# Modulation rows queued behind the feed-forward's weights, and a first stage cut into quarters of the contraction

## Chip, cores and metric

The kernel runs on one core of one Trainium2 chip, in one launch. The metric is device time in microseconds. Times inside the profile are counted from the start of the span of one profiled execution.

## What is computed

Two transformer blocks over 256 tokens of width 1024, in fp32 accuracy. The first block has two layers; in each, a modulation (adaLN) vector made from a condition `c` scales and shifts the normed input:

```python
def adaln(cond, w_mod, b_mod):
    m = jnp.dot(jax.nn.silu(cond), w_mod) + b_mod
    return jnp.split(m[..., None, :], 6, axis=-1)
...
for l in range(DEPTH):                        # DEPTH = 2
    sh1, sc1, g1, sh2, sc2, g2 = adaln(c, w_mod[l], b_mod[l])
    csh1, csc1, cg1, csh2, csc2, cg2 = adaln(c_ctx, w_mod[l], b_mod[l])
    h = modulate(rms_norm(x, norm1_g[l]), sh1, sc1)
    hc = modulate(rms_norm(xc, norm1_g[l]), csh1, csc1)
    q, k, v, up, ca, cb = project_inputs(h, w_in[l], q_norm_g[l], k_norm_g[l])
...
    mix = jnp.concatenate([attn, pool_o, conv_o], axis=-1)
    x = x + g1 * jnp.einsum('blm,md->bld', mix, w_out[l])
    x = x + g2 * swiglu(modulate(rms_norm(x, norm2_g[l]), sh2, sc2), w_ffn_in[l], w_ffn_out[l])
```

Here `modulate(h, shift, scale)` is `h * (1 + scale) + shift`, and `w_mod[l]` is 1024 by 6144. Layer 0 does the same for the context `xc`. The second block (four gated branches) is the same in both kernels.

## The kernel before

**Layout.** Activations lie feature-major: 8 tiles of 128 features, with 512 columns (256 context tokens, 256 tokens). Every product is made of three fp32r matmuls (`mm3`, L353 to L355): high times high, high times low, low times high. `weights` loads a chunk of 512 KB into one of 4 `wraw` buffers (an issue on SP), rounds it on ScalarE (`whi`, L343) and takes the rest on VectorE (`wlo`, L344); `whi` and `wlo` have 3 buffers each.

**Order.** The program is traced in order, and a scheduler then orders each engine's instructions by the readiness that it works out at build time and by priority (earlier in the trace is higher). Work that waits for nothing can so be moved far ahead of its place. `tc.issue_after(i)` holds every instruction traced in its block on i's engine, and only there, behind i in that engine's queue.

**First stage of layer 0.** `modulation` makes a group of 1024 modulation columns: 8 chunks of `w_mod` (128 rows by 1024 columns, 512 KB), four matmuls of 256 columns for each (L507), then a copy, two transposes (L514) and additions of the bias. Groups 0 and 1 hold shift and scale of features 0 to 511 and 512 to 1023. `first_norm(0)` makes group 0 and norms features 0 to 511 (`norm`, L489 to L492). Then `feats` runs the first three of the four products of the convolution's input (`ab`, each 128 columns by the whole contraction) over the first half of the contraction, with the steps of `first_norm(1)` in between, and over the second half after it. The fourth product follows alone. The row of reciprocal norms that `norm` needs comes from L431 to L474.

**Rest of the modulation.** Layer 0's other three PE groups lie in `queue`; `fill` steps them from `each`, twice for each of the first 12 of 16 attention units, with the lower priority `LATE`. Layer 0's last part and all six of layer 1 come from `modulation_by_rows` on VectorE: a transposed chunk of `w_mod` (512 KB, in one of 2 `wmod` buffers) is multiplied with the row of silu(c) and summed (L567), for each of up to two conditions, after the condition's rows have been loaded and put through Silu (L559). It is a generator that is stepped three times for each feed-forward unit of layer 0; one step is one chunk with all its conditions, 56 steps in all.

**After attention** come the merge (`project_rows`, L867 and L881, with L835 as the residual), the second norm (L442, L446, L489 to L492), and the feed-forward in thirds of 8, 7 and 7 units.

Of the kernel before, what the change touches and what calls it, by code (L numbers as in the profile page):

```python
# [39 lines left out]

MOD_GROUPS = {0: ((4, 5, 0, 1), (6, 7, 2, 3)) + tuple(tuple(range(4 * i, 4 * i + 4)) for i in (2, 4, 3))}
# [12 lines left out]
def _weight_plan():  # L54
# [7 lines left out]
    for l in range(DEPTH):  # L62
        for g, parts in enumerate(MOD_GROUPS.get(l, ())):
            cols = np.concatenate([np.arange(c * 256, c * 256 + 256) for c in parts])
            for k in range(8):
                rows(("mod", l, g, k), "w_mod", (l,), cols, k * 128, 1)
        for which in range(6):
# [17 lines left out]
        for j in range(4):  # L85
# [190 lines left out]
def tile_two_blocks(ctx: ExitStack, tc: tile.TileContext, w: bass.AP, blk: bass.AP, cols: bass.AP,  # L276
# [61 lines left out]
    def weights(key):  # L338
# [4 lines left out]
        act.copy(out=hi[:, :m], in_=t[:, :m])  # L343
        dve.tensor_tensor(lo[:, :m], t[:, :m], hi[:, :m].bitcast(F32), op=ALU.subtract)  # L344
# [24 lines left out]
    def feats(items, h, spans, between=None, p="mm"):  # L369

# [4 lines left out]
        turns = [range(KD)] if between is None else [range(KD // 2), range(KD // 2, KD)]  # L375
        behind = None
        n = 0
        for a, b in spans:
            for ks in turns:
                if ks[0]:  # L380
                    behind = None
                for (wH, wL), t in zip(ws, ps):
                    for k in ks:
                        with tc.issue_after(behind.ins) if behind else nullcontext():
                            mm3(t[:, a - lo:b - lo], (wH[:, k], wL[:, k]), (h[0][:, k, a:b], h[1][:, k, a:b]),
                                k == 0, k == KD - 1)
                        n += 1
                        if between and n in STEPS:
                            for _ in range(STEPS[n]):
                                behind = next(between, behind)  # L390
# [86 lines left out]
    def norm(h, lo, hi, parts, ks=range(KD), row=None, wide=False):  # L477

        ps, bc = row or rows_of_rstd(lo, hi)
        for k in ks:  # L480
            for a, b, sc, sh in parts:
# [9 lines left out]
                act.activation(hi_, t, AF.Identity, bias=sh[:, k:k + 1])  # L491
                dve.scalar_tensor_tensor(lo_, t, sh[:, k:k + 1], hi_.bitcast(F32), op0=ALU.add,  # L492
# [6 lines left out]
    modv = {l: const.tile([128, 6, KD, 2], F32, name=f"modv{l}") for l in range(DEPTH)}  # L499

# [43 lines left out]
    def fill(n):  # L544
# [3 lines left out]
        for _ in range(n):  # L548
            while queue and next(queue[0], None) is None:
# [1092 lines left out]
```

## Time and profile before

| what | us |
|---|---|
| three runs | 1454.83, 1464.14, 1463.14; median 1463.14 |
| profiled execution, device time | 1457.94 |
| its span, first to last instruction | 1455.8 |
| PE busy in the span | 1367.4 (94%) |
| VectorE, ScalarE, GpSimd busy | 959.2, 623.2, 233.3 |

PE is TensorE's matmul queue. Busy time of PE is modelled from starts; what counts is where PE stands idle and at which granted clock it runs (PEclk 1.00 is 2.4 GHz, 0.50 would be 1.2 GHz throughout; its mean over the span is 0.957). 2.1 us of the device time lie outside the span.

### The profile page before, as it was taken

The numbers are of one execution on the slowest core, as the hardware profiler recorded it, in microseconds if no ns is written. First come the engines' busy times: TensorE is split into PE (matmuls) and PEld (weight loads), VectorE is DVE, ScalarE is ACT, GpSimd is POOL, SyncE is SP. The second block draws the span as 40 slices with busy tenths as digits, with TensorE's granted clock in tenths as the row PEclk, the third lists the DMA queues.
The fourth block names the chain that finished last, engine by engine and source line by source line (L and its number), as shares of the span: only waits on it lengthen the run. The fifth ranks groups of instructions, "written<-read, shape, count | busy, mean of one in ns | idle before, by whom it ended". The sixth has DMA issues, their size and how long they took to land. (4 is left out here: it accounts for less than half of the span.)

```text
span 1455.8 us, 22714 instructions
## 1 busy us (share of the span) xinstructions
PE 1367.4 (94%) x8750; PEld 1195.1 (82%) x8750; DVE 959.2 (66%) x1924; ACT 623.2 (43%) x1100; POOL 233.3 (16%) x274
## 2 busy tenths in 40 slices
PE   5999989879999999998988989999989998999999
PEld 2699656778878888888967889999967887988999
DVE  4598659998784333335986755555695676657565
ACT  3333464242212222324444544434654559446443
POOL 0055530230000000003416210000362002000000
PEclk9999977989999999999978999999998999999999
DMA  9632533437773223222321335555642423434553
GB/s 341 227 127 92 191 137 107 159 118 259 261 251 124 95 95 102 96 92 74 124 80 44 103 130 189 177 186 178 235 150 94 153 84 109 133 109 150 184 181 129
DMA packets 61308, 213.51 MB, mean 147 GB/s; under 512 B 6928, under 2 KB 8080, under 8 KB 60944
## 3 DMA queue, kind: packets, MB, share of 16 engines
q1 hardware_dynamic: 60768, 209.90, 42.6%
q10 hardware_dynamic: 432, 2.16, 0.4%
q8 instruction: 69, 1.13, 0.3%
q14 instruction: 39, 0.32, 0.1%
HBM read 210.98 MB, written 1.05 MB: 146 GB/s over the span
## 5 line engine op out<-in xcount | busy, mean ns | idle before, releaser
L343 ACT CAST whi<-wraw 128x1024 fp32r<-128x1024 f32 (+2 forms) x296 | 304.7, 1033 | 515.5 <-PE ps_mm L354 256.6
L344 DVE TENSOR_TENSOR wlo<-wraw,whi 128x1024 fp32r<-128x1024 f32 (+2 forms) x296 | 360.6, 1220 | 181.9 <-ACT whi L343 179.2
L353 PE MATMUL ps_mm<-hH,whi 128*128 128x256 f32 (+1 forms) x1056 | 345.0, 330 | 10.4 <-ACT hH L491 7.3
L354 PE MATMUL ps_mm<-hL,whi 128*128 128x256 f32 (+1 forms) x1056 | 343.1, 326 | 1.9 <-DVE hL L492 1.9
L355 PE MATMUL ps_mm<-hH,wlo 128*128 128x256 f32 (+1 forms) x1056 | 342.2, 325 | 1.3 <-DVE wlo L344 1.3
L353 PEld LDWEIGHTS ps_mm<-hH,whi 128*128 128x128 f32 x1056 | 204.6, 195 | 32.3 <-ACT hH L491 9.1
L353 PE MATMUL ps_mm<-hidH,whi 128*128 128x256 f32 (+1 forms) x683 | 216.9, 320 | 7.7 <-ACT hidH L349 4.8
L354 PEld LDWEIGHTS ps_mm<-hL,whi 128*128 128x128 f32 x1056 | 205.1, 194 | 19.6 <-DVE hL L492 3.4
L355 PEld LDWEIGHTS ps_mm<-hH,wlo 128*128 128x128 f32 x1056 | 204.9, 194 | 17.1 <-DVE wlo L344 1.9
L354 PE MATMUL ps_mm<-hidL,whi 128*128 128x256 f32 (+1 forms) x683 | 216.2, 317 | 2.4 <-DVE hidL L350 2.3
L355 PE MATMUL ps_mm<-hidH,wlo 128*128 128x256 f32 (+1 forms) x683 | 215.3, 317 | 0.1
L354 PE MATMUL ps_mm<-wlo,hH 128*128 128x256 f32 (+2 forms) x464 | 145.8, 316 | 4.9 <-DVE wlo L344 4.9
L353 PEld LDWEIGHTS ps_mm<-hidH,whi 128*128 128x128 f32 x683 | 130.3, 192 | 17.8 <-ACT hidH L349 5.7
L353 PE MATMUL ps_mm<-whi,hH 128*128 128x256 f32 (+2 forms) x464 | 141.2, 313 | 2.0 <-ACT tm L634 1.5
L355 PE MATMUL ps_mm<-whi,hL 128*128 128x256 f32 (+2 forms) x464 | 142.9, 310 | 0.0
L354 PEld LDWEIGHTS ps_mm<-hidL,whi 128*128 128x128 f32 x683 | 130.9, 192 | 12.2 <-DVE hidL L350 3.5
L355 PEld LDWEIGHTS ps_mm<-hidH,wlo 128*128 128x128 f32 x683 | 130.5, 192 | 8.7 <-DVE wlo L344 0.5
L567 DVE CUSTOM_DVE_ANT_0 ps_md<-wmod,tm 128x512 f32<-128x512 f32 x160 | 114.7, 717 | 21.8 <-DMA wmod<-in_w_dram 19.9
L464 POOL TENSOR_TENSOR squares<-squares,scr 128x256 f32<-128x256 f32 (+1 forms) x28 | 31.6, 1129 | 567.3 <-ACT scr L463 566.9
L358 POOL TENSOR_TENSOR st<-st,mhalf 128x4 f32<-128x4 f32 (+3 forms) x54 | 69.3, 1289 | 224.0 <-DVE st L619 95.8
L354 PEld LDWEIGHTS ps_mm<-wlo,hH 128*128 128x128 f32 x464 | 89.6, 193 | 13.4 <-DVE wlo L344 7.6
L353 PEld LDWEIGHTS ps_mm<-whi,hH 128*128 128x128 f32 x464 | 88.7, 193 | 7.4 <-ACT tm L634 1.6
(346 smaller groups left out, 1996.4 us busy)
## 6 DMA issues: line engine op xcount, KB each, us to landing
wraw<-in_w_dram SPq DMA_DIRECT2D x271, 512.0 KB, 3.4
wmod<-in_w_dram SPq DMA_DIRECT2D x85, 512.0 KB, 4.0
wraw<-in_w_dram SPq DMA_DIRECT2D x32, 448.0 KB, 3.2
xT<-in_x_dram ACTq DMA_DIRECT2D x2, 1024.0 KB, 6.8
single<-in_w_dram SPq DMA_DIRECT2D x8, 256.0 KB, 7.6
wraw<-in_w_dram SPq DMA_DIRECT2D x4, 288.0 KB, 3.2
tm<-in_rows_dram SPq DMA_DIRECT2D x4, 256.0 KB, 6.0
out_dram<-scr SPq DMA_DIRECT2D x8, 128.0 KB, 1.7
```

Of the source, the lines that this page charges most:

```text
L343: act.copy(out=hi[:, :m], in_=t[:, :m])
L344: dve.tensor_tensor(lo[:, :m], t[:, :m], hi[:, :m].bitcast(F32), op=ALU.subtract)
L353: pe.matmul(ps, a[0], b[0], start=start, stop=False)
L354: pe.matmul(ps, a[0], b[1], start=False, stop=False)
L355: P["product"] = pe.matmul(ps, a[1], b[0], start=False, stop=stop)
L358: pool.tensor_tensor(t, t, mhalf[:, :n], op=ALU.pow)
L464: eng.tensor_tensor(squares[:, lo:hi], squares[:, lo:hi], q, op=ALU.add)
L567: dve.tensor_tensor_reduce(bank("md"), t[:, i * 512:i * 512 + 512], crow[2 * j + i], 1.0, 0.0, ALU.mult, ALU.add, sums[j][:, i * KD + d:i ...
```

## The change

- The first stage goes by quarters of the contraction. The first two modulation groups are replaced by four parts (`first_modulation`), each with shift and scale of 256 features: 4 chunks of two row blocks by 512 columns (512 KB), eight matmuls of 128 columns for each chunk, one copy, one transpose. The four `ab` products take their weights as four chunks of 256 rows by 512 columns (`abq`) and accumulate in four banks side by side. After the products of each of a quarter's two feature tiles, two chunks of the next part are stepped, behind the last product on PE (`P["product"]`).
- The first weights after that stage are rounded and split behind the last norm of it (`P["behind"]`), and `layer_scalars` is held behind the same norm and the last product.
- `fill` is held behind the last product traced before it.
- The rows on VectorE: one step is one chunk with one condition (80 steps). They are stepped three times for each feed-forward unit and once for each output tile of the feed-forward's projection, VectorE's part behind the last weights' split (`P["split"]`), the loads behind the last load (`P["load"]`).

```diff
-ROWS_PER_STEP = 3
+ROWS_PER_STEP = (3, 1)
-STEPS = {1: 1, 2: 1, 3: 1, 4: 1, 5: 1, 6: 1, 7: 1, 8: 1, 11: 9}
-MOD_GROUPS = {0: ((4, 5, 0, 1), (6, 7, 2, 3)) + tuple(tuple(range(4 * i, 4 * i + 4)) for i in (2, 4, 3))}
+MOD_GROUPS = {0: tuple(tuple(range(4 * i, 4 * i + 4)) for i in (2, 4, 3))}
...
+        if l == 0:
+            for q in range(4):
+                cols = np.arange(q * 256, q * 256 + 256)
+                for k in range(0, 8, 2):
+                    rows(("first", q, k), "w_mod", (l,), np.concatenate([D + cols, cols]), k * 128, 2)
+                rows(("abq", q), "w_in", (l,), np.arange(1792, 2304), q * 256, 2)
...
-        act.copy(out=hi[:, :m], in_=t[:, :m])
-        dve.tensor_tensor(lo[:, :m], t[:, :m], hi[:, :m].bitcast(F32), op=ALU.subtract)
+        with ExitStack() as order:
+            for i in P.pop("behind", ()):
+                order.enter_context(tc.issue_after(i.ins))
+            act.copy(out=hi[:, :m], in_=t[:, :m])
+            P["split"] = dve.tensor_tensor(lo[:, :m], t[:, :m], hi[:, :m].bitcast(F32), op=ALU.subtract)
...
+    def first_modulation(q, pools, p):
+        ps = bank(p)
+        for k in range(0, KD, 2):
+            t = raw_chunk(("first", q, k), next(pools))[0]
+            for i in range(2):
+                for g in range(4):
+                    o = i * 512 + g * 128
+                    pe.matmul(ps[g * 32:g * 32 + 32, :128], csil[:, k + i, :], t[:, o:o + 128],
+                              start=(k + i == 0), stop=(k + i == KD - 1), tile_position=(0, g * 32))
+            yield
+        cp = P["wk"].tile([128, 256], F32, name="cp")[:, :128]
+        act.copy(out=cp, in_=ps[:, :128])
+        pe.transpose(ps[:, 256:384], cp, ident)
...
-        for _ in range(n):
-            while queue and next(queue[0], None) is None:
-                queue.pop(0)
+        with tc.issue_after(P["product"].ins):
+            for _ in range(n):
+                while queue and next(queue[0], None) is None:
+                    queue.pop(0)
...
+    def rows_step(i):
+        with tc.issue_after(P["split"].ins), tc.issue_after(P["load"].ins):
+            for _ in range(ROWS_PER_STEP[i]):
+                next(rows, None)
...
-                if d < KD - 1:
-                    yield
+                    if d < KD - 1 or j < js[-1]:
+                        yield
...
+    def first_products(items):
+        pools = cycle(("wraw", "wraw", "wmod"))
+        ps = [bank("mm" if i < 3 else "sc") for i in range(4)]
+        mods = [first_modulation(q, pools, ("md", "sc")[q % 2]) for q in range(4)]
+        for q in range(4):
+            wH, wL = weights(("abq", q))
+            for _ in mods[q]:
+                pass
+            norm(h, 0, 512, parts(0, 0, scale1, (0, 1)), range(2 * q, 2 * q + 2), row, True)
+            for k in range(2):
+                for (key, _), t in zip(items, ps):
+                    c = slice(key[2] * 128, key[2] * 128 + 128)
+                    mm3(t, (wH[:, k, c], wL[:, k, c]), tuple(x[:, 2 * q + k] for x in h), q + k == 0, q + k == 4)
+                if q < 3:
+                    with tc.issue_after(P["product"].ins):
+                        next(mods[q + 1])
+                        next(mods[q + 1])
+        P["behind"] = P["normed"], P["rest"]
+        for (_, evac), t in zip(items, ps):
+            evac(t)
...
-        layer_scalars(l)
+        with tc.issue_after(P["normed"].ins), tc.issue_after(P["rest"].ins), tc.issue_after(P["product"].ins):
+            layer_scalars(l)
...
-                if not last:
-                    for _ in range(ROWS_PER_STEP):
-                        next(rows, None)
+                rows_step(0)
...
             project_rows(l, range(KD), lambda d: (weights(("fo", l, t, d)), hs), range(f1 - f0), 5, final, 1, lo,
-                         after2 if final else None)
+                         after2 if final else None, lambda: rows_step(1))
```

## Rows read from the trace of the kernel before

**Rows 1.** Windows: us; PE, PEld, DVE, ACT, POOL busy (count); PEclk; DMA share; GB/s.

```profile
190.00:200.00 10.00, 7.21 (x42) 5.19 (x34) 2.08 (x6) 9.87 (x20) 6.91 (x10) 0.67 0.50 181
200.00:210.00 10.00, 10.00 (x30) 5.52 (x28) 6.80 (x20) 3.82 (x11) 0.00 (x0) 0.68 0.01 2
...
280.00:300.00 20.00, 13.66 (x95) 12.13 (x93) 19.94 (x48) 6.95 (x13) 7.04 (x8) 0.96 0.49 166
300.00:320.00 20.00, 18.37 (x121) 18.12 (x122) 20.00 (x52) 7.09 (x16) 10.48 (x10) 0.78 0.29 99
...
340.00:360.00 20.00, 20.00 (x90) 16.57 (x89) 16.88 (x42) 6.18 (x8) 0.00 (x0) 1.00 0.77 259
...
660.00:680.00 20.00, 16.73 (x130) 16.33 (x129) 10.78 (x21) 7.72 (x15) 6.76 (x8) 0.94 0.33 107
680.00:700.00 20.00, 19.44 (x143) 18.89 (x142) 16.93 (x32) 12.66 (x22) 9.56 (x8) 0.89 0.26 83
```

**Rows 2.** Instructions of L567 over the whole span; duration ns, first and last start.

```profile
L567 DVE CUSTOM_DVE_ANT_0 ps_md<-wmod,tm x160: 683/699/1730, 202.7 to 440.0; 128x512 f32<-128x512 f32 x160
L567 DVE DVE_READ_ACCUMULATOR2_ANT st<- x160: 133/140/146, 203.3 to 440.6; 128x1 f32 x160
...
  DMA wmod<-in_w_dram: 19.9, 20
```

**Rows 3.** Instructions of L559 over the whole span.

```profile
L559 ACT ACTIVATE tm<-tm x4: 629/630/637, 187.1 to 195.9; 128x512 f32<-128x512 f32 x4
L559 ACT ACT_TABLE_LOAD  x3: 1283/1283/1283, 185.8 to 194.6; - x3
```

**Rows 4.** Timeline of PE, 150 to 240: start, us, line, operation, count, idle before.

```profile
157.54 0.38 PE L353 MATMUL ps_sc<-hidH 64*128 64x256 f32 x1
...
170.23 0.39 PE L355 MATMUL ps_sc<-hidH,hidL 64*128 64x512 f32 x1
...
189.74 1.08 PE L507 MATMUL ps_md<-wmod,csil 128*32 128x256 f32 x8 [3.44 <-DMA wmod<-in_w_dram]
...
200.22 0.79 PE L353 MATMUL ps_sc<-hidH 64*128 64x512 f32 x1
...
232.28 0.62 PE L355 MATMUL ps_sc<-hidH,hidL 64*128 64x512 f32 x1
```

**Rows 5.** Timeline of PE, 262 to 310.

```profile
290.35 0.39 PE L353 MATMUL ps_mm<-hidH,whi 128*128 128x256 f32 x1 [1.48 <-DVE xT L835]
...
298.10 0.77 PE L446 MATMUL ps_aux<-scr,ones 128*128 128x256 f32 x2 [3.72 <-DVE scr L442]
...
301.22 0.80 PE L353 MATMUL ps_mm<-hH,whi 128*128 128x256 f32 x2 [2.36 <-ACT hH L491]
```

**Rows 6.** Groups of VectorE by line, 280 to 325: busy us, mean ns, idle before.

```profile
L567 DVE CUSTOM_DVE_ANT_0 ps_md<-wmod,tm 128x512 f32<-128x512 f32 x30 | 24.1, 805 | 0.1
```

**Rows 7.** Timeline of PE and ACT, 19 to 66.

```profile
19.75 2.08 PE L446 MATMUL ps_aux<-scr,ones 128*128 128x512 f32 x2
...
23.06 0.37 ACT L512 COPY cp<-ps_sc 128x256 f32<-128x256 f32 x1 [0.60 <-PE ps_sc L507]
...
27.26 0.50 PE L353 MATMUL ps_mm<-hH,whi 128*128 128x512 f32 x1 [3.34 <-ACT hH L491]
...
46.47 0.64 PE L507 MATMUL ps_md<-wmod,csil 128*32 128x256 f32 x8
...
64.23 0.39 PE L354 MATMUL ps_mm<-hL,whi 128*128 128x512 f32 x1
64.46 0.39 PE L355 MATMUL ps_mm<-hH,wlo 128*128 128x512 f32 x1
```

**Rows 8.** Window 20 to 40; columns as in Rows 1.

```profile
20.00:40.00 20.00, 14.42 (x87) 6.37 (x88) 10.64 (x25) 7.41 (x13) 0.35 (x1) 0.83 0.94 323
```

**Rows 9.** Groups of PE by line and shape, 0 to 64.

```profile
L507 PE MATMUL ps_md<-wmod,csil 128*32 128x256 f32 x32 | 3.0, 389 | 0.0
```

**Rows 10.** The page's costliest groups.

```profile
L344 DVE TENSOR_TENSOR wlo<-wraw,whi 128x1024 fp32r<-128x1024 f32 (+2 forms) x296 | 360.6, 1220 | 181.9 <-ACT whi L343 179.2
```

More of the change, by code (lines that the diff above doesn't have):

```diff
@@ L84, in _weight_plan @@
             rows(("up", l, j), "w_in", (l,), np.arange(1536 + j * 128, 1664 + j * 128), 0, 8)
-        for j in range(4):
+        for j in range(4 if l else 0):
             rows(("ab", l, j), "w_in", (l,), np.arange(1792 + j * 128, 1920 + j * 128), 0, 8)
@@ L367, in st, with feats @@
         return P["wk"].tile([128, n], F32, name=f"st{n}", bufs=8 if n < 64 else 3)
-    def feats(items, h, spans, between=None, p="mm"):
+    def feats(items, h, spans, p="mm"):
         ws = [weights(key) for key, _ in items]
@@ L374, in feats @@
         lo, hi = min(a for a, b in spans), max(b for a, b in spans)
-        turns = [range(KD)] if between is None else [range(KD // 2), range(KD // 2, KD)]
-        behind = None
-        n = 0
         for a, b in spans:
[L379 to L390, printed above, removed]
+            for (wH, wL), t in zip(ws, ps):
+                for k in range(KD):
+                    mm3(t[:, a - lo:b - lo], (wH[:, k], wL[:, k]), (h[0][:, k, a:b], h[1][:, k, a:b]),
+                        k == 0, k == KD - 1)
         for (key, evac), t in zip(items, ps):
@@ L490, in norm @@
                 hi_, lo_ = h[0][:, k, a:b], h[1][:, k, a:b]
[L491 to L492 removed]
+                P["normed"] = act.activation(hi_, t, AF.Identity, bias=sh[:, k:k + 1])
+                P["rest"] = dve.scalar_tensor_tensor(lo_, t, sh[:, k:k + 1], hi_.bitcast(F32), op0=ALU.add,
                                          op1=ALU.subtract)
@@ L845, in tile_two_blocks, with project_rows @@
     h = new_h()
-    pools = cycle(("wraw", "wraw", "wmod"))
-    def first_norm(half):
-        yield from modulation(0, half, pools, "sc")
-        norm(h, 0, 512, parts(0, 0, scale1, (0, 1)), range(half * 4, half * 4 + 4), row, True)
-    for _ in first_norm(0):
-        pass
-    def project_rows(l, d_list, make, ks, which, final, first_half, lo, after):
+    def first_products(items):
[18 more added lines that the diff above has]
+            evac(t)
+    def project_rows(l, d_list, make, ks, which, final, first_half, lo, after, each=None):
         late = d_list[-3:] if lo == 0 and final else ()
@@ L870, in project_rows @@
                 after(d, lo, 512)
+            if each:
+                each()
         if not late:
@@ L883, in project_rows @@
                 after(d, s * 256, s * 256 + 256)
+    rows = modulation_by_rows()
     for l in range(DEPTH):
@@ L891, in tile_two_blocks @@
         if not last:
-            queue.extend(modulation(0, g) for g in range(2, 5))
+            queue.extend(modulation(0, g) for g in range(3))
         mix = {}
@@ L975, in tile_two_blocks @@
         project_rows(l, range(KD), lambda d: merge(1, d), range(4), 2, True, 0, lo, after)
-        rows = modulation_by_rows() if not last else None
         for t, (f0, f1) in enumerate(THIRDS):
```

14 lines of the change are left out of this document (12 added, 2 removed).

## Prediction

> **What bounds the kernel now.** I read the page's busy times first, then windows of 20 us over the span, then the waits and the timeline wherever PE was not full. PE is busy 94% of the span, so time is won only where PE idles or runs at the low clock. The steady feed-forward is not such a place: from 340 to 360 PE shows 20.00 of 20 at clock 1.00, although VectorE is at 16.88 and carries modulation rows [rows 1]. The rows are L567: 160 instructions of 0.70 us with 160 reads of 0.14 us, 134 us of VectorE in all, started from 202.7 to 440.0 [rows 2]. Their place in the trace is the feed-forward, yet they begin in the middle of attention: the scheduler used them as filler. Silu of the condition went along: four Silu and three table loads between 185.8 and 196.5, among the exponentials [rows 3]; each return to Exp is another load.
>
> Four places lose PE time. (a) From 190 to 200 PE is busy 7.21 of 10 at clock 0.67 while ScalarE is at 9.87; just before, PE stands 3.44 us at a queued modulation matmul whose chunk has not landed [rows 1, 4]. (b) From 200 to 233 attention runs with rows between its VectorE steps, at clock 0.68 [rows 1, 4]. (c) From 280 to 320 VectorE is 99.7% busy and PE loses 8.0 us (6.34 and 1.63); the chain of the second norm waits 1.48, 3.72 and 2.36 us [rows 1, 5], and 24.1 us of VectorE there are rows [rows 6]. (d) The first stage, which ends at 64.9 [rows 7].
>
> **(a) Silu and the fills.** Silu moves into the feed-forward, whose gate uses the same function. The three loads of 1.283 us, as many back to Exp, and 4 times 0.63 us leave ScalarE's queue, 10.2 us in all [rows 3]. PE can get back at most its idle 2.8 us, the wait of 3.44 us, and half of the low-clock time: clock 0.67 means that 66% of 10 us ran at 1.2 GHz, so 3.3 us. Sum 9.5; the floor is 0, if attention's chain fills the gap. I take 4, since the DMA wait may only move: the fills stay two for each unit, but now behind the unit's product instead of wherever the scheduler put them. Behind a waiting fill the unit's own matmuls still stand. Their loads are issued ahead on SP, one unit before, so I expect less waiting, not more.
>
> The Trainium skill (ScalarE: Activation LUTs, section "What ACT_TABLE_LOAD costs") adds a drain of about 1.38 us to each load, 2.66 us for a switch. Between the starts of the first and the third Silu load lie four switches (two to Silu, two back), 10.6 us by that figure, more than the 8.8 us that the rows leave; the rows speak for 1.28.
>
> **(b) Rows out of attention.** From 157.54 to 170.62 eight score products, four units, take 13.1 us: 3.3 us for a unit, without rows. From 200.22 to 232.90 twelve, six units, take 32.7 us, 5.4 for a unit [rows 4]. The excess of 2.1 us times six is 12.6 us, and the rows do not part its causes: matmuls of pooling and of the convolution's norm that stand in the second stretch, PE at 1.2 GHz, and attention's steps standing behind rows of 0.84 us. If it is only the first two, the gain is 0. I take a third, 4.
>
> **(c) Rows out of the norm.** After the change a row's VectorE part stands behind the split of the last weights traced, and the fourth weights of the feed-forward need one of three `whi` buffers, so no row can come before the first products. What remains is like the boundary from layer 0 to layer 1, which has no rows: 660 to 700 loses 3.27 and 0.56 us [rows 1]. Against 8.0 that gives 4.1 us. Low clock: 8% and 44% of 20 us before (10.4 us), 12% and 22% there (6.8 us); half the difference is 1.8 us. Sum 5.9. GpSimd's additions of squares then show up, as they do there, so I take 5; bounds 3 and 8.
>
> **(d) First stage by quarters.** Bytes and products stay: 16 chunks of 512 KB, 96 products. Products start 0.23 us apart [rows 7], so a quarter's 24 cost 5.5 us. A chunk was eight matmuls of 256 columns, 0.64 us [rows 7]; now it is sixteen of 128 columns. It costs between the same (columns decide) and twice that, 1.28 (instructions decide); I take 0.9, nearer to the row, so 3.6 us for a part. At each seam PE has nothing else: the part's last chunk is queued behind the quarter's last product, and copy, transpose, bias, scale and norm must follow. Before, copy to first product took 4.2 us (23.06 to 27.26), with a weight split of 1.2 us on VectorE in the way [rows 7, 10]; now that split lies under the products. I take 3.0. A quarter is 5.5 + 3.6 + 3.0 = 12.1; three and a last 5.5 make 41.8.
>
> The start: only a quarter's modulation (2 MB instead of 4) stands ahead, so the row of norms decides. Its broadcast L446 ended at 21.8 [rows 7]; the norm's two passes and the rounding, an estimated 0.9 us, put the first product at 22.7, against 27.26. End: 64.5 against 64.9. Before, the stage also did four fill steps (32 matmuls, 3.0 us) [rows 9], which now go into attention, where PE has idle time. Against this stands the clock: before, after an idle of 3.34 us, 20 to 40 ran at 0.83 [rows 7, 8], 34% of 20 us low, 3.4 us lost. Three seams of 3 us may each cost half of that or all. I set 3 us won against 3 us lost: 0, bounds 6 us won and 17 lost (below). The evacuations now come together at the end; the first finishes its Sigmoid under the other three products, so a bank is free in time. `layer_scalars` and the first split behind the last norm delay nothing that PE wants at once.
>
> **(e) Where the rows go.** 80 steps: three for each of 7, 7 and 7 units, and one for each projection tile: 29 by the end of the first third, 58 by the end of the second, 80 early in the last projection. The gate needed first (16 steps) is ready before the first projection. One unit gets 3 times 1.68 = 5.0 us of VectorE where before it got up to 10. Loads per unit on SP are 1.5 to 3 as before, with the same two buffers, and the four small loads of the condition's rows go along; a row waiting for its load now holds up the next weight split. Before, VectorE stood so 20 times, 19.9 us in all [rows 2], and PE stayed full [rows 1]. Cost 0; if that cover went, up to 3.
>
> **Sum.** 4 + 4 + 5 + 0 - 0 = 13 us. From the profiled execution's 1457.9 this gives 1445. That execution lies 5.2 us under the median of the three runs; the four executions average 1460.0, and from this I predict 1447. They spread over 0.64%, so 1% is about what can be told from no change.
>
> **Rivals.** *Attention is set by PE at 1.2 GHz.* Then (b) gives nothing and (a) only about 2: 7 us, 1453. For it: PE shows 10.00 of 10 from 200 to 210 at 0.68. Against it: from 190 to 200 the clock is as low with PE idle for 28% of the time, so there it follows the waiting and not the reverse [rows 1].
>
> *The seams keep the clock low (slower).* If PE runs from the second quarter on at 1.2 GHz, 72 products cost 0.23 us more each (16.6), and the eight chunks between them 0.9 more each (7.2): 23.8 us, less the 6 that an early start and the moved fills can win, so 17 net (rounded down). Against 13 won elsewhere that is 4 slower: 1464. It decides once the extra passes 19 us, four fifths of that. For it: 3.72 us of idle at 298 is followed by 0.78 in the next window [rows 1, 5]. Against it: each quarter holds 9 us of unbroken products. The Trainium skill (TensorE: Matmul & The Clock Gate, section "Why this matters for your kernels") warns against idle gaps between bursts of matmuls because they return the engine to its low clock; it speaks against this change at three seams, and no row here shows gaps repeated like this.
>
> *Attention returns to 2.4 GHz.* With Silu and rows gone, units take near 3.3 us again from 185 on: (a) and (b) give some 16 of their 22 us, (c) its 5, and the time is 1439. For it: four units ran so until 170 [rows 4]. Against it: the second stretch also holds other matmuls that stay.
>
> *The hold does nothing*, because the scheduler still finds room for rows early: then at most (a)'s fills count, 4 us, 1456. The fourth weights' wait for a buffer speaks against it.
>
> **Chances.** Forecast 0.50 (1440 to 1453), attention set by the clock 0.20, seams 0.12, attention at full clock 0.13, hold without effect 0.05. The range runs from 1434 (full clock and a good first stage) to 1463. More than 1% faster is below 1448.5 against the median and below 1445.4 against the mean of the four; between these, the forecast's range lies below in about half of its cases (0.27), and the full-clock case adds 0.13: 0.40. Slower by over 1% needs the seams at their worst and little won elsewhere: 0.06. Within 1%: 0.54.
>
> **What would show it.** Right: L567 starts after the first feed-forward product and runs to the end of layer 0; no table load for Silu among the exponentials; PE idle from 280 to 320 halved; first product before 24; three gaps of about 3 us in the first stage. Wrong: the stage ending later than 68 or its windows under clock 0.9; PE waiting on `wlo` in the feed-forward; attention as long as before with VectorE free.

## The result, and the profile after

The changed kernel takes 1442.24 us (median of 1445.26, 1442.25, 1442.22 and 1440.2), against 1459.12 of the kernel before beside it on the chip: ratio 0.9885, 95% interval 0.984 to 0.993. Its profiled execution has a span of 1443.5 us, 12.3 less than before's 1455.8.

Where they went is read from five starts on PE's timeline that both kernels have. Of the kernel before, first qk product, first merge product, and the first sum of squares of layer 1 (the first product at 27.26 and the first feed-forward product at 301.22 stand in [rows 7, 5]):

```profile
64.69 0.40 PE L353 MATMUL ps_mm<-whi,hH 128*128 128x256 f32 x2
...
236.93 1.42 PE L353 MATMUL ps_mm<-hidH,whi 128*128 128x512 f32 x1
...
666.68 0.28 PE L431 MATMUL ps_aux<-ones,squares 128*128 128x1 f32 x2
```

Of the changed kernel, the same view, with the transposes (L510) and first products (L361) of the first stage's quarters. A seam is PE's wait between a quarter's transpose and its first product, here 3.58, 5.61 and 1.91 us:

```profile
24.52 0.50 PE L361 MATMUL ps_mm<-hH,whi 128*128 128x512 f32 x1 [1.99 <-ACT hH L487]
...
28.82 0.95 PE L505 MATMUL ps_sc<-wraw,csil 128*32 128x128 f32 x16
29.59 0.61 PE L505 MATMUL ps_sc<-wmod,csil 128*32 128x128 f32 x16
30.13 0.50 PE L361 MATMUL ps_mm<-hH,whi 128*128 128x512 f32 x1
...
34.60 0.33 PE L510 MATMUL ps_sc<-first,cp 128*128 128x128 f32 x1 [0.44 <-ACT cp L509]
38.50 1.65 PE L361 MATMUL ps_mm<-hH,whi 128*128 128x512 f32 x3 [3.58 <-ACT hH L487]
...
49.06 0.33 PE L510 MATMUL ps_md<-first,cp 128*128 128x128 f32 x1 [0.44 <-ACT cp L509]
55.00 1.65 PE L361 MATMUL ps_mm<-hH,whi 128*128 128x512 f32 x3 [5.61 <-ACT hH L487]
...
65.84 0.33 PE L510 MATMUL ps_sc<-first,cp 128*128 128x128 f32 x1 [0.44 <-ACT cp L509]
68.08 0.97 PE L361 MATMUL ps_mm<-hH,whi 128*128 128x512 f32 x3 [1.91 <-ACT hH L487]
...
74.19 0.39 PE L361 MATMUL ps_mm<-whi,hH 128*128 128x256 f32 x1
...
162.74 0.45 PE L731 MATMUL ps_aux<-first,e 128*128 128x128 f32 x1 [2.10 <-DVE hidL L358]
...
239.15 0.79 PE L361 MATMUL ps_mm<-hidH,whi 128*128 128x512 f32 x1
291.56 0.38 PE L361 MATMUL ps_mm<-hH,whi 128*128 128x256 f32 x1 [2.19 <-ACT hH L487]
```

Layer 1 begins at 651.39. From start to start:

| stretch, us | before | after | difference |
|---|---|---|---|
| to the first product | 27.26 | 24.52 | -2.7 |
| first stage, to the first qk product | 37.43 | 49.67 | +12.2 |
| attention, to the first merge product | 172.24 | 164.96 | -7.3 |
| merges and second norm, to the first feed-forward product | 64.29 | 52.41 | -11.9 |
| feed-forward of layer 0 | 365.46 | 359.83 | -5.6 |
| the rest of the span | 789.1 | 792.1 | +3.0 |

The change is two changes with opposite signs. With the rows away from attention and the norm, three stretches win 24.8 us; the first stage by quarters ends 9.5 us later than before. The last row holds none of the moved work (of the edits only the hold on layer 1's `layer_scalars` reaches it): over all the profiled executions below that part takes 788 to 797 us, with and without that hold.

Windows of the changed kernel, columns as in [rows 1]:

```profile
20.00:40.00 20.00, 13.99 (x104) 8.96 (x97) 9.19 (x23) 6.64 (x13) 0.00 (x0) 0.82 0.59 207
40.00:60.00 20.00, 13.95 (x99) 10.34 (x97) 5.60 (x14) 3.03 (x6) 1.52 (x3) 0.76 0.66 214
...
160.00:180.00 20.00, 17.71 (x100) 11.76 (x92) 12.92 (x31) 9.11 (x30) 10.97 (x22) 0.66 0.49 164
180.00:200.00 20.00, 19.27 (x122) 11.65 (x120) 11.58 (x23) 8.62 (x25) 9.22 (x16) 1.00 0.50 177
200.00:220.00 20.00, 18.50 (x123) 11.32 (x122) 13.07 (x35) 9.88 (x30) 6.05 (x9) 1.00 0.41 136
...
280.00:300.00 20.00, 17.48 (x116) 16.78 (x115) 12.87 (x26) 10.19 (x21) 11.17 (x12) 0.83 0.36 135
300.00:320.00 20.00, 20.00 (x142) 18.75 (x141) 13.72 (x27) 9.62 (x17) 4.29 (x4) 1.00 0.21 67
```

From 180 to 220 the clock is 1.00, where before had 0.67 and 0.68 from 190 to 210 [rows 1]; from 280 to 320 PE loses 2.52 us instead of 8.0 and VectorE has room. Against that, 20 to 60 stands at 0.82 and 0.76, and attention has a fall of its own: 0.66 from 160 to 180, behind the wait of 2.10 us at 162.74.

The rows, L595, over the span, and the Silu of the condition, L587:

```profile
L595 DVE CUSTOM_DVE_ANT_0 ps_md<-wmod,tm x160: 689/699/702, 313.7 to 612.7; 128x512 f32<-128x512 f32 x160
...
  DMA wmod<-in_w_dram: 9.9, 13
```
```profile
L587 ACT ACTIVATE tm<-tm x4: 631/632/633, 278.0 to 281.3; 128x512 f32<-128x512 f32 x4
```

The hold works: no row before 313.7, and none in the last 38 us of layer 0. The Silus run in the second norm, with no table load of their own.

### The profile page after: what moved, and what is told of

Its sections match the earlier page's. It is cut to its first block, busy times and chain, and to the rows that moved or that the text cites. A ratio compares the mean times of both kernels' runs of the same rounds, so it can differ in the third digit from the quotient of the medians.

```text
span 1443.5 us, 22992 instructions
## 1 busy us (share of the span) xinstructions
PE 1360.8 (94%) x8878; PEld 1197.9 (83%) x8878; DVE 965.6 (67%) x1928; ACT 614.5 (43%) x1094; POOL 237.8 (16%) x274
## 5 line engine op out<-in xcount | busy, mean ns | idle before, releaser
L361 PE MATMUL ps_mm<-hH,whi 128*128 128x256 f32 (+1 forms) x1056 | 344.3, 330 | 18.9 <-ACT hH L487 16.9
L361 PEld LDWEIGHTS ps_mm<-hH,whi 128*128 128x128 f32 x1056 | 204.3, 195 | 39.5 <-ACT hH L487 19.6
L361 PE MATMUL ps_mm<-hidH,whi 128*128 128x256 f32 (+1 forms) x683 | 214.8, 317 | 3.0 <-ACT hidH L357 1.7
L361 PE MATMUL ps_mm<-whi,hH 128*128 128x256 f32 (+2 forms) x464 | 141.1, 313 | 2.0 <-ACT tm L662 1.5
L361 PEld LDWEIGHTS ps_mm<-hidH,whi 128*128 128x128 f32 x683 | 129.2, 190 | 12.0 <-ACT hidH L357 1.9
L595 DVE CUSTOM_DVE_ANT_0 ps_md<-wmod,tm 128x512 f32<-128x512 f32 x160 | 111.5, 697 | 12.7 <-DMA wmod<-in_w_dram 9.9
L863 DVE SCALAR_TENSOR_TENSOR xT<-ps_mm,modv,xT 128x256 f32<-128x256 f32 x116 | 52.6, 480 | 72.5 <-PE ps_mm L363 72.4
```

Source lines behind the costliest of these rows:

```text
L361: pe.matmul(ps, a[0], b[0], start=start, stop=False)
L595: dve.tensor_tensor_reduce(bank("md"), t[:, i * 512:i * 512 + 512], crow[2 * j + i], 1.0, 0.0, ALU.mult, ALU.add, sums[j][:, i * KD + d:i ...
L863: dve.scalar_tensor_tensor(xT[:, d, r], ps[:, s * 256 - lo:s * 256 - lo + 256], M(l, which, 1 - s)[:, d:d + 1], xT[:, d, r], op0=ALU.mult, ...
```

## Experiments

Each kernel is timed beside the kernel before; "stage", "attention", "norm" and "FFN" are the stretches of the table above in its one profiled execution, "wait" is the longest idle of PE within attention that the timeline shows, and "at 0.50" is how much of attention ran at that granted clock, in us, from windows cut where the clock changes.

| kernel | median us | ratio (95%) | stage ends | attention | wait | at 0.50 | norm | FFN | span |
|---|---|---|---|---|---|---|---|---|---|
| before | 1459.12 | 1 | 64.69 | 172.24 | 3.44 | 33.9 | 64.29 | 365.46 | 1455.8 |
| after | 1442.24 | 0.9885 (0.984 to 0.993) | 74.19 | 164.96 | 2.10 | 20.5 | 52.41 | 359.83 | 1443.5 |
| rows_only | 1428.25 | 0.9803 (0.9781 to 0.9824) | 64.15 | 155.53 | 1.42 | 4.2 | 52.82 | 360.09 | 1424.9 |
| quarters_only | 1476.87 | 1.0148 (1.0108 to 1.0188) | 80.65 | 177.98 | 2.68 | 43.0 | 65.30 | 368.54 | 1485.5 |
| rows_fill | 1431.23 | 0.9818 (0.979 to 0.9846) | 62.73 | 160.84 | 1.32 | 19.6 | 55.99 | 360.22 | 1429.9 |
| abq_early | 1443.72 | 0.9907 (0.9876 to 0.9938) | 73.22 | 162.62 | 2.18 | 21.9 | 56.39 | 360.51 | 1443.9 |
| silu_back | 1440.98 | 0.9884 (0.9827 to 0.9941) | 64.08 | 167.70 | 2.06 | 27.3 | 53.99 | 359.77 | 1441.4 |
| rows_norm | 1447.35 | 0.9928 (0.9898 to 0.9958) | 64.28 | 157.49 | 1.83 | 13.7 | 65.21 | 366.14 | 1441.2 |
| hidden | 1434.12 | 0.9837 (0.9782 to 0.9892) | 60.46 | 162.20 | 2.18 | 25.3 | 53.40 | 359.63 | 1430.5 |
| after_unheld | 1445.07 | 0.9917 (0.9888 to 0.9947) | 79.47 | 163.53 | 1.98 | 18.9 | 52.22 | 359.80 | 1443.5 |
| hidden_free | 1431.57 | 0.9832 (0.9792 to 0.9872) | 61.75 | 158.10 | 1.32 | 12.7 | 54.41 | 358.73 | 1422.8 |
| hidden_unheld | 1433.75 | 0.9834 (0.9788 to 0.9881) | 64.96 | 167.29 | 1.83 | 28.1 | 52.67 | 358.29 | 1440.3 |
| silu_once | 1437.58 | 0.9863 (0.982 to 0.9905) | 64.42 | 166.93 | 2.07 | 27.3 | 53.97 | 359.76 | 1434.4 |
| rows_only_again | 1434.03 | 0.9826 (0.9793 to 0.9859) | 64.26 | 154.47 | 1.39 | 0.4 | 55.68 | 359.35 | 1430.1 |

### The two halves of the change

**rows_only**: the kernel before with the rows' part of the diff.

```diff
-ROWS_PER_STEP = 3
+ROWS_PER_STEP = (3, 1)
...
-                if not last:
-                    for _ in range(ROWS_PER_STEP):
-                        next(rows, None)
+                rows_step(0)
...
+            if each:
+                each()
```

`rows_step(0)` is three steps, `each` in `project_rows` is `rows_step(1)`, one step; both stand behind the last split and load.

> The kernel before with the rows alone changed: begun behind the feed-forward's weights, three steps a pair and one an output tile; its first stage and its unheld fill steps stay. If the parts add up (theory: the rows won about 25 us and the first stage by quarters gave back about 9.5 of it), the first qk product stays at 64.7 us, the first feed-forward product comes 15 to 25 us earlier than before's 301.2, and the whole takes 1434 to 1444 us, faster than the changed kernel or level with it. If the prediction's sum was right piece by piece (rows and Silus 13, first stage 0), it takes about 1446 us. If the hold on the fill steps was the larger part of the gain in attention, attention stays as long as before (172 us from first qk product to first merge product) and only the 8 to 12 us of the second norm are won: about 1449.

Measured 1428.25 us, faster than the changed kernel, and more than the 25 us of the first theory. Its windows:

```profile
160.00:180.00 20.00, 18.58 (x134) 11.86 (x131) 12.89 (x31) 7.56 (x25) 11.50 (x28) 1.00 0.50 165
180.00:200.00 20.00, 18.90 (x125) 12.87 (x122) 16.00 (x35) 12.44 (x38) 12.11 (x15) 1.00 0.32 101
200.00:220.00 20.00, 16.01 (x83) 11.47 (x81) 15.46 (x41) 13.22 (x41) 2.02 (x2) 0.89 0.00 1
```

Attention stays at 1.00 nearly to its end and takes 155.53 us, 16.7 less than before; the norm wins 11.5 and the feed-forward 5.4.

**quarters_only**: the changed kernel with the rows and the fill steps as before.

```diff
-        with tc.issue_after(P["product"].ins):
-            for _ in range(n):
+        for _ in range(n):
...
-                rows_step(0)
+                if not last:
+                    for _ in range(ROWS_PER_STEP):
+                        next(rows, None)
```

> The changed kernel with before's rows (three steps a pair, free to run ahead into attention) and its fill steps unheld: what is left of the change is the first stage by quarters. If the seams are a loss that nothing returns, the first qk product comes 6 to 10 us later than before's 64.7 and the whole is slower by that: 1465 to 1469 us. If the prediction's term was right (0, within 6 won and 17 lost, the seams paid by the earlier first product), 1459. If the later end of the first stage is given back in attention because the rows and the fill steps that ran inside the first stage before now find time there, between the two, and attention is shorter by what the stage is longer.

Measured 1476.87, slower by 1.5%: the first stage by quarters alone is a loss, and nothing returns it. That is more than the 1465 to 1469 expected. The stage ends 16.0 us later than before's, not 6 to 10, with seams of 5.51 and 6.24 us and a fill step in front of the last quarter that stands 3.28 us for its chunk. (The profiled execution, 1487.30, is the slowest of the four.) The product of the two halves' ratios, 0.9948, is above the whole change's 0.9885; neither half has the hold on the fill steps, which the next two runs look at.

**rows_fill**: rows_only with the hold on the fill steps.

```diff
-        for _ in range(n):
-            while queue and next(queue[0], None) is None:
+        with tc.issue_after(P["product"].ins):
+            for _ in range(n):
+                while queue and next(queue[0], None) is None:
```

> The kernel before with the rows changed and the fill steps of the modulation held behind the products, its first stage as before. If the parts add up: first qk product near 65 us, first feed-forward product near 282 (before's 301.2 less about 7 in attention and 12 in the norm), and the whole 1430 to 1436 us, about 9 us faster than the changed kernel. If the first stage by quarters costs nothing, or frees attention of fill steps that are back here, it is level with the changed kernel, 1440 to 1446. The difference from the kernel with the rows alone is what the hold on the fill steps is worth: 0 to 4 us.

Measured 1431.23; its interval overlaps with that of rows_only. In the profiled execution the stage ends 1.4 us earlier and attention is 5.3 us longer, with a stretch at 0.50 that begins 14 us after PE's last wait:

```profile
193.70:210.80 17.10, 17.10 (x83) 9.65 (x84) 7.50 (x22) 5.63 (x19) 0.00 (x0) 0.50 0.33 110
```

The hold brings this kernel nothing that can be measured in the whole.

**after_unheld**: the changed kernel without that hold (the same lines the other way).

> The changed kernel with the hold on the fill steps taken away, so that they may run as soon as their chunk has landed. Without the rows' change the unheld fill steps stood in the first stage's gaps and it ended at 80.7 us instead of 74.2. If they do so here too, the stage ends near 80 and the whole takes 1445 to 1450: the hold is worth its 4 to 8 us to a first stage by quarters, though the kernel with the first stage of before had nothing from it (1431 with, 1428 without). If the hold costs attention what it did there (5 us, by the loads that come just before their use), the two cancel, and the whole is level with 1442.

Measured 1445.07, level with the changed kernel within the intervals. The stage ends at 79.47, as expected; a fill step stands in it for 3.44 us. The 5.3 us are back by the end of the span (1.4 in attention, 3.6 behind layer 0, where the fill steps no longer run). So the hold shortens this first stage, but its worth in the whole isn't shown.

### What in the rows cost attention

**silu_back**: rows_only with the four Silus among the exponentials, where before had them.

```diff
+                for i in {16: (0, 1), 17: (2,), 18: (3,)}.get(P["exps"], ()):
+                    with tc.issue_after(exp.ins):
+                        P["silu"] = silu_crow(i)
```

> The kernel with the rows alone changed (1428 us, attention 155.5 us from the first qk product to the first merge product), with only the four Silus of the condition's rows put back to where the kernel before had them: two behind the 16th exponential of layer 0, one behind the 17th, one behind the 18th, so that six table loads come back; the rows' sums stay in the feed-forward. If the Silus and table loads with the stall behind them (and the low clock that follows it) are what cost attention its 16.7 us, attention goes back to about 168 to 172 and the whole to 1441 to 1445. If the sums on VectorE were the larger part, attention stays within 4 us of 155.5 and the whole at 1430 to 1433. The prediction had 4 us for each: 159.5.

Measured 1440.98, attention 167.70: 12.2 of the 16.7 us are back, with no row on VectorE. Timeline of PE:

```profile
186.56 0.71 PE L727 MATMUL ps_aux<-tm,aT 128*128 128x128 f32 x4 [2.06 <-ACT aT L724]
...
189.08 1.08 PE L507 MATMUL ps_md<-wmod,csil 128*32 128x256 f32 x8 [1.38 <-DMA wmod<-in_w_dram]
...
192.79 0.58 PE L353 MATMUL ps_sc<-hidH 64*128 64x256 f32 x1 [1.69 <-ACT e L704]
```

and windows:

```profile
180.00:200.00 20.00, 14.12 (x81) 9.10 (x73) 7.32 (x16) 18.34 (x37) 10.96 (x14) 0.69 0.42 156
200.00:220.00 20.00, 19.87 (x81) 13.94 (x81) 11.66 (x32) 8.62 (x26) 1.02 (x1) 0.67 0.00 0
```

ScalarE is busy 18.34 of 20, and PE waits three times for more than a microsecond. The clock is 0.50 from 187.8 to 204.9, 12 us beyond the end of the last of these waits: the low clock outlasts the stall. The 0.67 of the second window is not one stretch, however. The clock is 1.00 again from 204.9 to 211.7 and 0.50 once more from 211.7 to 221.9; PE's only idle time from 200 to 220 is 0.13 us at 211.95.

**silu_once**: the same, all four Silus behind the 16th exponential, two table loads in place of six.

```diff
-                for i in {16: (0, 1), 17: (2,), 18: (3,)}.get(P["exps"], ()):
+                for i in {16: range(4)}.get(P["exps"], ()):
```

> The kernel with the rows alone changed, with the four Silus of the condition's rows put back behind the 16th exponential of layer 0 in one group: two table loads among the exponentials in place of the six that cost 12.2 us. If the cost goes by the table loads and Silus themselves, a third to a half of it stays: attention 159.5 to 161.5 us, the whole 1432 to 1434. If it goes by one stall long enough for TensorE's clock to fall (the wait after the first table load was 2.06 us), most of it stays: attention 163 to 168, the whole 1436 to 1441. If only several stalls in a row bring the clock down, nothing is seen: 155.5 to 157.

Attention 166.93, 11.4 of the 12.2 us. Timeline of PE:

```profile
188.46 0.71 PE L727 MATMUL ps_aux<-tm,aT 128*128 128x128 f32 x4 [2.07 <-ACT aT L724]
...
191.53 1.08 PE L507 MATMUL ps_md<-wmod,csil 128*32 128x256 f32 x8 [1.92 <-DMA wmod<-in_w_dram]
```

the windows behind them, cut where the clock changes, and from PE's timeline what it runs ahead of the last one:

```profile
190.70:204.30 13.60, 12.78 (x45) 7.35 (x45) 3.71 (x12) 6.14 (x18) 6.42 (x10) 0.50 0.10 41
204.30:211.10 6.80, 6.80 (x40) 5.12 (x40) 4.26 (x11) 2.39 (x6) 1.02 (x1) 1.00 0.00 0
211.10:221.40 10.30, 10.30 (x43) 8.11 (x41) 6.16 (x18) 6.18 (x22) 0.00 (x0) 0.50 0.00 0
```
```profile
207.95 1.84 PE L431 MATMUL ps_mm<-ones,scr 128*128 128x1 f32 x16
```

A third of the table loads leaves nearly all of the cost, so the price does not go by the loads. The first of these stretches at 0.50 follows the stall behind the first load and the chunk's wait after it. The second, three quarters as long, follows no wait: PE was busy throughout. Ahead of it stand the sixteen sums of squares of the convolution's norm, matmuls of one column that count as busy. In rows_only other matmuls part them, and the clock stays at 1.00 until 215.4:

```profile
196.78 0.35 PE L431 MATMUL ps_mm<-ones,scr 128*128 128x1 f32 x2 [0.57 <-ACT scr L827]
...
197.85 0.73 PE L431 MATMUL ps_mm<-ones,scr 128*128 128x1 f32 x6
...
198.96 0.95 PE L431 MATMUL ps_mm<-ones,scr 128*128 128x1 f32 x8
```

No run changes that order alone, so how much of the 11.4 us the Silus' stall owns, and how much the order of these sums, isn't shown. The whole, 1437.58, is 3.5 us above rows_only_again beside it, and those intervals overlap.

**rows_norm**: the kernel before with the rows held behind the last exponential.

```diff
+                    with tc.issue_after(P["exp"].ins):
+                        for _ in range(ROWS_PER_STEP):
+                            next(rows, None)
```

> The kernel before with the rows (Silus, loads and sums) held behind the last exponential of layer 0 but free from there, so that they run in the merges and the second norm and not among the exponentials. If attention and the norm lose separately, attention is 155 to 158 us, as with the rows changed, and the stretch from the first merge product to the first feed-forward product stays at 60 to 66 us, as in before's 64.3 (52.8 with the rows changed): 1438 to 1442 in all. If the norm's 11.5 us came from the low clock that attention handed on, that stretch falls to about 55 too, and the whole is near 1431.

`P["exp"]` is on ScalarE, so the hold is on the Silus, and the sums wait for them. Attention 157.49, norm 65.21: the two lose separately, and the norm's loss is the rows that run in it. Groups of VectorE in that stretch (222 to 287):

```profile
L567 DVE CUSTOM_DVE_ANT_0 ps_md<-wmod,tm 128x512 f32<-128x512 f32 x46 | 35.2, 766 | 1.7 <-ACT tm L559 1.0 <-DMA wmod<-in_w_dram 0.2
```

The feed-forward took 366.14 too, as before, so its 6 us go with the burst as well. The median of 1447.35 lies above the forecast and above the profiled execution's own 1443.37; the ten executions reach from 1441.06 to 1453.56.

### What the seams cost

**abq_early**: the changed kernel, weights of the next quarter's products called for earlier.

```diff
+        ahead = weights(("abq", 0))
...
-            wH, wL = weights(("abq", q))
+            wH, wL = ahead
...
+                    if k == 0:
+                        ahead = weights(("abq", q + 1))
```

> The changed kernel with each quarter's weights for the products (load, cast and split) called for one quarter ahead, before the last chunks of the next modulation quarter. If the cast behind its late load is what made the second seam 5.6 us (it began at 53.5, 2.6 us after the engine was free, with three activations of the norm behind it), that seam falls to about 3 us and the first from 3.6 to about 3; the stage ends some 3 us earlier, near 71, and the whole takes about 1439. If the chain of the norm itself (copy, transpose, bias, scale, norm, activation) is the bound, the seams stay within 0.5 us and so does the time. Loss is possible: the modulation's chunks come later on the queue by one load each, 0.9 us or more, and a seam starts later by that.

Seams on PE's timeline:

```profile
39.83 1.65 PE L361 MATMUL ps_mm<-hH,whi 128*128 128x512 f32 x3 [4.35 <-ACT hH L487]
...
52.06 0.97 PE L361 MATMUL ps_mm<-hH,whi 128*128 128x512 f32 x3 [1.91 <-ACT hH L487]
...
64.39 1.65 PE L361 MATMUL ps_mm<-hH,whi 128*128 128x512 f32 x3 [1.91 <-ACT hH L487]
```

The second seam falls from 5.61 to 1.91, so the late cast was its excess. The first grows to 4.35: its cast still waits for the load, until 38.32. Together the seams are 2.9 us shorter, but the stage ends only 1.0 earlier and the time is that of the changed kernel, not 1439: the first product is 0.5 later, and the last quarter, which began at full clock in the changed kernel (three products in 0.97) and lasted 6.1 us, begins here at 1.2 GHz (1.65) and lasts 8.8.

**hidden**: the changed kernel with the next quarter's chain under this quarter's products.

```diff
+                    with tc.issue_after(P["turned"].ins) if k and i > 1 else nullcontext():
...
+                n = q + 1 + k
+                with tc.issue_after(P["product"].ins):
+                    if n < 4:
+                        next(mods[n])
+                        next(mods[n])
+                    if k == 0 and q < 3:
+                        ahead = weights(("abq", q + 1))
+                        ready(q + 1)
```

`ready` is the rest of a part's modulation and its norm; `P["turned"]` is the part's transpose, behind which the last two of the four products of the second half stand.

> The changed kernel with its quarters overlapped: the weights for the next quarter's products and the copy, transpose, bias, scale and norm of the next quarter are called for after the products of the first half of a quarter, its transpose stands in the middle of the second half's products, and the chunks of the quarter after that behind them. If the chain in the seam is the loss (seams of 3.6, 5.6 and 1.9 us and, behind each, some ten products at 1.2 GHz), the gaps fall to under 1.5 us each, the first qk product comes at 60 to 65 us instead of 74.2 and the whole takes 1428 to 1434. If the loads are the bound (five chunks of 512 KB a quarter through six buffers), PE waits for DMA in place of the norm, and the stage ends at 68 or later.

Measured 1434.12. Timeline of PE:

```profile
36.67 0.98 PE L361 MATMUL ps_mm<-hH,whi 128*128 128x512 f32 x3 [0.84 <-ACT hH L487]
...
46.33 0.96 PE L361 MATMUL ps_mm<-hH,whi 128*128 128x512 f32 x3 [1.19 <-ACT hH L487]
...
54.33 0.96 PE L361 MATMUL ps_mm<-hH,whi 128*128 128x512 f32 x3 [0.53 <-ACT hH L487]
```

With gaps of about a microsecond every quarter after the first starts at full clock, and the stage ends at 60.46: 13.7 us before the changed kernel's and 4.2 before the old one's. PE waits for no load there. So the quarters are not the loss; the seams are.

**hidden_free** and **hidden_unheld**: hidden, fill steps held only behind the first stage, or not at all.

```diff
-        with tc.issue_after(P["product"].ins):
+        with tc.issue_after(P["stage"].ins):
...
+        P["stage"] = P["product"]
```

`P["stage"]` is the last product of the first stage; hidden_unheld has no `with` there.

> The kernel with overlapped quarters (first stage over at 60.5 us, attention 162.2), with its fill steps held only behind the last product of the first stage and free from there. If attention's length is set by whether a wait of some 2 us lets TensorE's clock fall (none above 1.42 us where the rows alone are changed: clock 1.00 and 155.5 us; one of 2.18 us with the fill steps held: clock 0.50 for the next 10 us and 162.2 us), free fill steps cover that wait, attention takes 155 to 158 us, and the whole 1423 to 1427, faster than the kernel with the rows alone changed. If the length of attention hangs on which waits the order happens to leave and not on the hold, it stays at 160 to 165 and the whole at 1430 to 1434.

> The kernel with overlapped quarters and no hold on the fill steps at all: three of them stand among the first stage's last products, and their chunks share its buffers. With seams of a microsecond there is little time to fill, so the first stage should end 2 to 4 us later than 60.5 (each step about 0.75 us, and the chunk that waits for its buffer); attention as with the hold behind the first stage, 155 to 158 us; the whole 1425 to 1431. If the fill steps stretch the stage by their loads, as they did the quarters without overlap (80.7 against 74.2), it ends at 66 or later and the whole takes 1432 or more.

hidden_free: attention 158.10, the whole 1431.57, above the 1423 to 1427 expected (six executions, 1424.56 to 1441.42; the profiled one is the fastest). hidden_unheld: the stage ends at 64.96 and attention takes 167.29, longer than with the hold; a fill step waited 1.83 us for its chunk at 159.16, and from 160 to 180 the clock was 0.50. So it is not the hold as such that makes attention long, and the theory of hidden_free is shown only in part: how attention fares depends on what the order leaves in it, and a wait is not all of that (see below).

**rows_only_again**: rows_only unedited, beside hidden_free.

> The kernel with the rows alone changed once more, beside the overlapped quarters on one chip: 1426 to 1431 us by its first runs. If the overlapped first stage is worth its 3.7 us at equal attention, this one is slower by 2 to 5 us than that; if fill steps or waits in attention take it back, the two are level or this one is faster.

Measured 1434.03 against 1431.57, ratios 0.9826 and 0.9832: level. The overlapped first stage ends 2.5 us earlier and attention is 3.6 longer in these two executions. No version is shown to beat rows_only. Against the changed kernel it is 8 to 14 us faster by the medians of its two sets of runs; the interval of the first set lies apart from the changed kernel's, that of the second overlaps it.

## Why the prediction held, and where its steps did not

The total was right: 13 us forecast, 1447 with a range down to 1434, measured 1442.24, some 5 us better. Its terms were not. The second norm and the feed-forward gave 12.5 us more than their terms, the first stage lost 9.5 that its term put at nothing. That these errors nearly cancel is luck.

**(a) Silu, 4 forecast: 12.2 in silu_back.** The direction was right, the size wrong, and beyond the bound of 9.5. That bound counted the idle time and the low clock from 190 to 200 alone, and I had put all that follows under (b). Before's clock is 0.50 from 196.2 to 206.4, behind the stall and the waits after it, 1.00 to 213.3, and 0.50 again to 223.5; silu_back and silu_once show the same two stretches with the rows gone. An estimate from silu_once's windows: the stretch right behind the stall is 13.6 us at half the clock, so some 7 us, and PE is idle 2.0 us longer than in rows_only. The second stretch, some 5 us by the same count, may not be the Silus'.

**(b) Rows out of attention, 4: 4.5.** What is left between silu_back (167.70) and before (172.24), a difference of two single executions. No run has the sums in attention without the Silus, so that this is their price isn't shown. The excess itself is 13.1 us, not 12.6, if it is not rounded first; the matmuls of the convolution's norm, which the prediction named among its causes, stand 0.5 us ahead of the fall at 213.3.

**What (a) and (b) gave in the changed kernel: 7.3, not 16.7.** It has a fall of its own in attention, behind the 2.10 us wait on `hidL`, which rows_only has not. The longest wait does not set attention's length: 1.32 us went with 158.10 and 160.84, 1.83 with 157.49 and 167.29. The time at 0.50 nearly does: at most 4.2 us where attention took 154.5 and 155.5, 13 to 14 where it took 157 to 158, 19 to 28 from 161 to 168, 34 and 43 at 172 and 178. An estimate from the same rows: less PE's idle time and half of its busy time at 0.50, attention is 142 to 148 us in all fourteen executions.

Some falls follow a wait of some 2 us. Others follow the sums of the convolution's norm: in eleven executions 12 to 16 of these stand in a row while the clock is at 1.00, and in ten it falls at most 2.6 us after the last (rows_fill at 193.7, hidden_free at 200.3, neither with a wait above 1.32). The changed kernel is the exception, with 14 in a row and no fall for 9.8 us. In both executions of rows_only they are parted and nothing falls there. That is a pattern and no experiment. Why an order leaves such a wait or such a row of sums, and whether the hold on the fill steps makes them likelier, stays open.

**(c) Rows out of the norm, 5 (3 to 8): 11.9.** rows_norm shows that it is the rows. The mechanism was right, the size wrong: PE's idle time between the first merge product and the first feed-forward product falls from 10.7 to 2.5 us, 8.2 in place of 4.1, and its clock there rises from 0.92 to 1.00. My count began at 280. The loss began earlier: 45 rows of before run in that stretch, not the 30 of [rows 6] alone, and PE waits 1.47 and 1.66 us on the last mix tiles at 265.69 and 268.31, the second time for a split of the convolution that stood behind a row. (VectorE was 99.9% busy from 280 to 320; the 99.7% is its first half alone.)

**(d) First stage by quarters, 0: 9.5 lost.** This step failed. Forecast end 64.5, measured 74.19. The first product came at 24.52, not 22.7 (+1.8). From there, 22.1 us of products as forecast; twelve chunks, in pairs of 1.01 to 1.31 us (28.82 to 30.13 is one), are 6.6 us in place of 10.8; three seams, transpose and its wait included, are 4.35, 6.38 and 2.68, 13.4 in place of 9.0; and what is left of the 49.67 us, 7.6, is nearly all products at 1.2 GHz, which I had set off, at 3, against the fill steps. My 3.0 for a seam is good for the third, where nothing else is queued. In the first two the weight cast stands in the norm's chain on ScalarE and waits for its load:

```profile
36.99 1.04 ACT L351 CAST whi<-wraw 128x1024 fp32r<-128x1024 f32 x1 [0.60 <-DMA wraw<-in_w_dram]
37.95 1.30 ACT L487 ACTIVATE hH<-tm,modv 128x256 fp32r<-128x256 f32 x3
...
53.50 1.04 ACT L351 CAST whi<-wraw 128x1024 fp32r<-128x1024 f32 x1 [2.64 <-DMA wraw<-in_w_dram]
54.45 1.30 ACT L487 ACTIVATE hH<-tm,modv 128x256 fp32r<-128x256 f32 x3
```

Three of the quarter's four activations stand behind a cast that is itself waiting for its load. I had written that the split lies under the products; it lies under them only if its load has landed, and the load was called for behind two chunks of the modulation.

**(e) Rows in the feed-forward, 0 (up to 3 lost): 5.6 won.** PE was idle for 3.7 us of before's feed-forward and for none of the changed kernel's; the rest of the 5.6 us isn't accounted for. The two longest waits stood behind rows on VectorE: four rows from 400.11, the first of which had waited 2.03 us for its chunk, run ahead of the product (L990) whose split ends the wait at 404.49, and three from 322.89 ahead of the split at 325.08 that ends the one at 326.35. rows_norm, which keeps these bursts, keeps the time. Before's waits, 301 to 667 (engine, line, releaser; total, times, longest), with the norm's own first:

```profile
PE ps_mm L353 <- ACT hH L491: 2.4, 1, 2.4
PE ps_mm L353 <- ACT hidH L349: 1.7, 1, 1.7
PE ps_mm L355 <- DVE wlo L344: 0.9, 1, 0.9
```

From 292 to 651 the changed kernel shows no wait of PE. I had read 340 to 360, full before and after, and taken it for the whole stretch.

**The rivals.** "Attention returns to 2.4 GHz" is what rows_only does; the changed kernel does it from 176 to 221, behind a fall of its own. "Attention is set by PE at 1.2 GHz" is half of the truth: the low clock was there and cost most, but it could be won back: with Silus and rows gone it went. "The seams keep the clock low" named the right place: the windows fell to 0.82 and 0.76 and the stage ended after 68, both set down as signs of error. Its price for the clock, 23.8 us, was too high against 7.6, since each quarter returned to 2.4 GHz after some ten products; the seams themselves, which it left at 3.0, were longer. The Trainium skill (TensorE: Matmul & The Clock Gate, section "Why this matters for your kernels") warns of idle gaps between bursts of matmuls; these rows agree, with products at 1.2 GHz behind the seams of 3.58 and 5.61 us, and with gaps of 0.53 to 1.19 us in hidden the loss is gone. "The hold does nothing" fell: no row came before 313.7.

## What to carry to other kernels

Price a stall by the low clock that follows it, not by its own length, and look for that clock in the windows behind the stall: here Silus with two table loads came with 11 us of attention, some 7 of them by the low clock right behind their stall. And do not take a busy PE for one that keeps its clock: matmuls of one column count as busy, and in ten executions of eleven the clock fell behind a dozen or more of them, though no run tests them alone. A stage cut into parts gains only if the next part's whole chain, its weights' load and cast included, runs under this part's products; cut without that, it paid each seam twice, in idle time and in slow products. And test the halves of a double change apart: the better half alone was 8 to 14 us faster than both together.

## What the chip showed beyond that

Short waits count. After PE's wait of 2.10 us at 162.74 the granted clock was 0.50 to 176.3; after waits of 2.07 and 1.92 us in silu_once it was 0.50 for 13.6 us, of which PE was busy for 12.78. But a wait is neither enough nor needed. At one place, 171.4 to 172.0, six executions wait 1.30 to 1.45 us: within 2 us behind it the clock fell in two of them (before at 172.3, silu_once at 173.6) and not in the other four. And at 193.7 in rows_fill and 211.1 in silu_once it fell with PE busy, behind 12 and 16 matmuls of one column. A later part of the kernel with none of the moved work in it moved by 9 us between executions (788 to 797), so a term of 4 us is read from its own stretch rather than from the whole.
